# Seven block products in place of eight in the gate and up products of a feed-forward layer

## The chip, the cores and the metric

The kernel runs on one core of a Trainium2 chip. The metric is the device time of one execution in microseconds: the median of three runs before the change is 3075.05 us (3074.8 to 3081.02). TensorE (PE) multiplies; a weight load (PEld) brings the stationary operand into it. VectorE (DVE) and ScalarE (ACT) work on PSUM and SBUF; SyncE (SP) issues every DMA of this kernel, in one queue and in program order.

## The reference, cut to what matters

Two trunk layers run over 1072 token columns (32 of the sample group, 16 meta tokens, 1024 of the prompt). Each layer is a token mixer followed by a SwiGLU feed-forward part, both between norms:

```python
D_MODEL = 1024
D_FF = 2816                      # 22 tiles of 128 features
def swiglu(x, w_gate, w_up, w_down):
    return (jax.nn.silu(x @ w_gate) * (x @ w_up)) @ w_down
...
x = x + rmsnorm(mix.astype(x.dtype), norm_mix_post[l])
ff = swiglu(rmsnorm(x, norm_ffn_pre[l]), ffn_w_gate[l], ffn_w_up[l], ffn_w_down[l])
x = x + rmsnorm(ff.astype(x.dtype), norm_ffn_post[l])
```

Everything is float32. The reference computes in that precision, and the kernel keeps it by splitting each operand in two parts.

## The kernel before, in words

**Layout.** Features lie on the partitions, tokens along the free dimension. The 1072 tokens are cut into three blocks of 304, 384 and 384 columns (`BLKS`). The normalised input of a product lies in SBUF as a high and a low part, `xh` and `xl`, eight tiles of 128 features each (`KD = 8`); weights come from DRAM as units of 128x1024 numbers (`raw`, two buffers) and are split into `wh` (a copy on ACT, L57) and `wl` (a subtraction on DVE, L58). `mm3` (L154 to L156) makes one 128x128 by 128xN product as three matmuls: high by high, low by high, high by low.

**Storage.** 29 strips of 128x1072 numbers are handed out and taken back by the program. Eight PSUM banks serve the products in turn.

**Feed-forward.** The 22 tiles of hidden features are done in eleven groups (`FFG`): the first has 3 tiles, the second 1, the other nine 2 each. For a group, `ffn_gu` makes for each token block the gate product and the up product of a tile (8 x 3 matmuls each), takes the silu on ACT (L249), multiplies on DVE (L251) and splits the result into the strips `hid` (L170, L171). Then `kblock` multiplies the group's hidden tiles with their rows of the down weights and adds the results to the eight accumulator strips `acc` (L273 on DVE; L271 on ACT in the first group). One tile therefore costs 144 matmuls for gate and up and 72 for down.

**Ends of a layer.** In the last group each token block is finished with gate, up and down before the next one. `side(b, acc)` then queues the norm of that block: `postnorm` (squares summed on ACT and DVE, one matmul by ones, L178, an inverse root, then two DVE passes with the residual from DRAM) and, where another layer part follows, `prenorm` (the same again, ending in the split into `xh` and `xl`). Block order is 0, 1, 2, in the last layer 1, 2, 0 (`LAST`).

**Order of work.** A main generator emits the products; a `Driver` advances queued side generators (norms, scans, the sample states' updates) by a rate per step of the main one. Behind it a scheduler sets, when the program is built, each engine's final order. The sample states' update of a mixer (`later`: `even_samples`, `odd_samples`) runs beside the feed-forward part that follows it: per sample one load, a few DVE operations, one matmul (L1233), an addition (L1234), one store (L1235); in `odd_samples` there are 32 samples and two buffers for them.

Of the kernel before, what the change touches and what calls it, by code (L numbers as in the profile page):

```python
# [26 lines left out]


class Weights:
    """Ordered stream of [128, 1024] weight units, each split into two float32r parts."""  # L30

    def __init__(self, core, seq):
        self.core, self.seq = core, seq
        self.pos, self.done = 0, 0
        self.ready = {}
        self.reserve = 0
        self.raw = {}
        self.rpos = 0

    def _load(self):  # L40
        c = self.core
        src = self.seq[self.rpos]
        r = c.raw_p.tile([P, 4 * VA], F32, tag="raw", name="raw")[:, :src.shape[-1]]
        c.nc.sync.dma_start(out=r, in_=src)
        self.raw[self.rpos] = r
        self.rpos += 1

    def pump(self, limit):
        """Prepare units until `limit` are ready beyond those taken."""
        c = self.core  # L50
        while self.done < len(self.seq) and self.done - self.pos < limit and len(c.free) >= 2 + self.reserve:
            while self.rpos < len(self.seq) and self.rpos <= self.done:
                self._load()
            r = self.raw.pop(self.done)
            hi, lo = c.strip(F32R, "wh"), c.strip(F32R, "wl")
            w = r.shape[-1]
            c.nc.scalar.activation(out=hi.t[:, :w], in_=r, func=AF.Copy)  # L57
            c.nc.vector.tensor_tensor(out=lo.t[:, :w], in0=r, in1=hi.t[:, :w].bitcast(F32), op=ALU.subtract)  # L58
            self.ready[self.done] = (hi, lo)
            self.done += 1  # L60
            if self.rpos < len(self.seq) and self.rpos <= self.done:
                self._load()
# [10 lines left out]
    def pos_need(self):  # L73
        while len(self.core.free) < 2:
            self.core.D.force()
# [11 lines left out]
class Core:  # L87
    def __init__(self, ctx, tc, I, O):
# [18 lines left out]
        self.oh = self.dram.tile([P, 16, T], F32, name="oh")  # L107
        self.ol = self.dram.tile([P, 16, T], F32, name="ol")
# [17 lines left out]
    # storage  # L126
# [14 lines left out]
    def ps(self, n=512):  # L141
        tags = ["mm0", "mm1", "mm2", "kt", "sc", "a0", "a1", "o"][:self.nps]
# [4 lines left out]
    nps = 8  # L147
    tables = False

    # arithmetic  # L150
    def mm3(self, out, w, x, first, last):
        nc = self.nc
        (wh, wl), (xh, xl) = w, x
        nc.tensor.matmul(out, lhsT=wh, rhs=xh, start=first, stop=False)  # L154
        nc.tensor.matmul(out, lhsT=wl, rhs=xh, start=False, stop=False)  # L155
        nc.tensor.matmul(out, lhsT=wh, rhs=xl, start=False, stop=last)  # L156
# [16 lines left out]
    def rstd(self, ss, n, inv=None, eps=EPS):  # L173
        """rsqrt(mean + eps) on all partitions of the summed squares ss [128, n]."""
# [15 lines left out]
    def lnexp(self, after=None):  # L190
        """Load the table set that serves both Ln and Exp; placed behind `after`."""
# [18 lines left out]
    def prenorm(self, acc, b, w):  # L210
# [5 lines left out]
        for k in range(KD):  # L216
            xn = self.tmp(n)
# [21 lines left out]
    # feed-forward  # L239
    def ffn_gu(self, units, hid, b):  # L240
# [3 lines left out]
        for i in range(len(units) // 2):  # L244
            pg = self.proj(units[2 * i], b)
            yield
            pu = self.proj(units[2 * i + 1], b)
            sg = self.tmp(n)
            nc.scalar.activation(out=sg, in_=pg, func=AF.Silu)  # L249
            hd = self.tmp(n)  # L250
            nc.vector.tensor_tensor(out=hd, in0=sg, in1=pu, op=ALU.mult)  # L251
            self.split(hd, hid[2 * i].t[:, c0:c0 + n], hid[2 * i + 1].t[:, c0:c0 + n])
            yield
# [1343 lines left out]
```

## Time and profile before

| | |
|---|---|
| median of three runs | 3075.05 us |
| span of the profiled execution, first to last instruction (its own time: the page gives no other) | 3072.7 us |
| PE busy | 3005.9 us, 98% |
| DVE busy | 1717.4 us, 56% |
| ACT busy | 1174.9 us, 38% |
| DMA queue q1, share of 16 engines | 28.4% |
| mean granted clock of TensorE | 0.989 |
| feed-forward of the first layer, first gate product to last down product | about 607 to 1409 us |
| feed-forward of the second layer | about 2259 to 3055 us |

A PE row of the profile shows how long one matmul was in the array, from its start to its modelled end. Matmuls are pipelined, so the next one starts long before that end: what a matmul costs in a full stream is the distance from start to start, which the windows give as a stretch of time divided by the number of matmuls that started in it.

### The profile page before, as it was taken

What the parts mean: (1) busy time and instruction counts of PE and PEld (TensorE: products, weight loads), DVE (VectorE), ACT (ScalarE), POOL (GpSimd) and SP (SyncE); (2) the same over time, 40 slices, a digit from 0 to 9 for tenths busy, and PEclk for the clock granted to TensorE, in tenths of its full rate; (3) what the DMA queues carried; (4) which work ended last, traced back from release to release, by engine and by line L of the source; (5) the groups of instructions that cost most, each with busy time, mean ns of one, the idle gap of its engine ahead of it and who ended that gap; (6) DMA issues with size and microseconds to landing.
All of it is one profiled execution on the core that took longest, in us unless ns stands there. A gap on an engine that the chain in (4) does not pass through costs nothing.

```text
span 3072.7 us, 47149 instructions
## 1 busy us (share of the span) xinstructions
PE 3005.9 (98%) x19042; PEld 2897.2 (94%) x19042; DVE 1717.4 (56%) x3387; ACT 1174.9 (38%) x2442; POOL 9.2 (0%) x47
## 2 busy tenths in 40 slices
PE   7999999999999999998999999999999999999997
PEld 7998989999999999998988898989999999999996
DVE  7645545753444333368887787775482444454336
ACT  6533435542111111145667575854353111111113
POOL 0000000000000000000000000000000000000000
PEclk9999999999999999999999999999999999999998
DMA  4120216221211111113344444366332122222103
GB/s 140 42 72 29 79 67 202 96 83 49 83 69 62 49 49 55 43 58 113 99 131 125 130 135 139 117 210 216 132 117 76 55 83 83 83 90 84 54 15 115
DMA packets 180202, 286.38 MB, mean 93 GB/s; under 512 B 24944, under 2 KB 135952, under 8 KB 179984
## 3 DMA queue, kind: packets, MB, share of 16 engines
q1 hardware_dynamic: 179984, 283.37, 28.4%
q8 instruction: 149, 2.44, 0.3%
q14 instruction: 69, 0.57, 0.1%
HBM read 217.18 MB, written 66.14 MB: 92 GB/s over the span
## 4 chain that ended last, share of the span: by engine, by line
PE 89%; DVE 5%; ACT 2%; DMA 2%; issue 2%; SPq 0%; DVEq 0%; ACTq 0%
PE ps L154 26%; PE ps L155 25%; PE ps L156 25%; DMA cumb<-cum_d 1%; PE ps L524 1%; PE ps L526 1%; PE ps L525 1%; PE b_a L1131 1%; PE b_o L678 1%; PE b_a L1177 1%; PE b_o L1179 1%; DVE t L206 1%; PE b_o L675 1%; PE b_a L659 1%; DVE acc L235 1%
## 5 line engine op out<-in xcount | busy, mean ns | idle before, releaser
L154 PE MATMUL ps<-xh,wh 128*128 128x384 f32 (+1 forms) x4152 | 1371.8, 331 | 10.4 <-ACT xh L170 6.5
L155 PE MATMUL ps<-xh,wl 128*128 128x384 f32 (+1 forms) x4152 | 1362.0, 328 | 7.6 <-DVE wl L58 7.6
L156 PE MATMUL ps<-xl,wh 128*128 128x384 f32 (+1 forms) x4152 | 1360.7, 328 | 0.0
L154 PEld LDWEIGHTS ps<-xh,wh 128*128 128x128 f32 x4152 | 784.7, 189 | 29.1 <-issue 11.1
L155 PEld LDWEIGHTS ps<-xh,wl 128*128 128x128 f32 x4152 | 784.2, 189 | 15.4 <-DVE wl L58 8.8
L156 PEld LDWEIGHTS ps<-xl,wh 128*128 128x128 f32 x4152 | 783.7, 189 | 4.0 <-issue 1.7
L57 ACT ACTIVATE wh<-raw 128x1024 fp32r<-128x1024 f32 (+1 forms) x225 | 238.1, 1058 | 581.3 <-PE ps L156 357.0
L58 DVE TENSOR_TENSOR wl<-raw,wh 128x1024 fp32r<-128x1024 f32 (+1 forms) x225 | 273.7, 1223 | 250.1 <-ACT wh L57 133.1
L154 PE MATMUL ps<-hid,wh 128*128 128x384 f32 (+1 forms) x1056 | 346.2, 328 | 15.6 <-DVE t L251 7.8
L155 PE MATMUL ps<-hid,wl 128*128 128x384 f32 (+1 forms) x1056 | 345.0, 327 | 0.0
L156 PE MATMUL ps<-hid,wh 128*128 128x384 f32 (+1 forms) x1056 | 344.5, 327 | 0.0
L251 DVE TENSOR_TENSOR t<-t,ps 128x384 f32<-128x384 f32 (+1 forms) x132 | 69.2, 526 | 477.1 <-PE ps L156 474.5
L273 DVE TENSOR_TENSOR acc<-acc,ps 128x384 f32<-128x384 f32 (+1 forms) x480 | 235.8, 525 | 122.1 <-PE ps L156 121.9
L154 PEld LDWEIGHTS ps<-hid,wh 128*128 128x128 f32 x1056 | 200.0, 189 | 18.3 <-DVE t L251 9.2
L155 PEld LDWEIGHTS ps<-hid,wl 128*128 128x128 f32 x1056 | 200.0, 189 | 1.1
L156 PEld LDWEIGHTS ps<-hid,wh 128*128 128x128 f32 x1056 | 199.8, 189 | 0.1
L170 ACT ACTIVATE hid<-t 128x384 fp32r<-128x384 f32 (+1 forms) x132 | 65.9, 500 | 331.0 <-DVE t L251 330.9
L249 ACT ACTIVATE t<-ps 128x384 f32<-128x384 f32 (+1 forms) x132 | 61.5, 467 | 289.0 <-PE ps L156 288.9
L206 DVE TENSOR_TENSOR t<-t 128x384 f32<-128x384 f32 (+1 forms) x168 | 88.8, 529 | 24.7 <-ACT t L205 16.6
L1037 DVE SCALAR_TENSOR_TENSOR xs<-cv,o_convw,xs 128x1040 f32<-128x1040 f32 x72 | 93.4, 1299 | 14.0 <-ACT xs L1035 12.9
L171 DVE TENSOR_TENSOR hid<-t,hid 128x384 fp32r<-128x384 f32 (+1 forms) x132 | 69.7, 529 | 42.0 <-ACT hid L170 41.0
L205 ACT ACTIVATE t<-acc 128x384 f32<-128x384 f32 (+1 forms) x168 | 77.1, 496 | 41.6 <-DVE acc L1360 20.3
(275 smaller groups left out, 2840.5 us busy)
## 6 DMA issues: line engine op xcount, KB each, us to landing
raw<-in_wg SPq DMA_DIRECT2D x44, 512.0 KB, 3.2
raw<-in_wu SPq DMA_DIRECT2D x44, 512.0 KB, 3.3
raw<-in_wd SPq DMA_DIRECT2D x44, 512.0 KB, 3.2
cumb<-cum_d SPq DMA_DIRECT2D x32, 512.0 KB, 5.7
raw<-in_od_x SPq DMA_DIRECT2D x24, 512.0 KB, 3.5
oh<-t SPq DMA_DIRECT2D x48, 192.0 KB, 2.0
ol<-t SPq DMA_DIRECT2D x48, 192.0 KB, 2.2
xh<-oh SPq DMA_DIRECT2D x12, 768.0 KB, 5.8
```

The lines of the kernel that those rows point to most:

```text
L57: c.nc.scalar.activation(out=hi.t[:, :w], in_=r, func=AF.Copy)
L58: c.nc.vector.tensor_tensor(out=lo.t[:, :w], in0=r, in1=hi.t[:, :w].bitcast(F32), op=ALU.subtract)
L154: nc.tensor.matmul(out, lhsT=wh, rhs=xh, start=first, stop=False)
L155: nc.tensor.matmul(out, lhsT=wl, rhs=xh, start=False, stop=False)
L156: nc.tensor.matmul(out, lhsT=wh, rhs=xl, start=False, stop=last)
L170: self.nc.scalar.activation(out=hi, in_=src, func=AF.Copy)
L171: self.nc.vector.tensor_tensor(out=lo, in0=src, in1=hi.bitcast(F32), op=ALU.subtract)
L205: nc.scalar.activation(out=sq, in_=acc[k].t[:, c0:c0 + n], func=AF.Square)
L206: nc.vector.tensor_tensor(out=ss, in0=ss, in1=sq, op=ALU.add)
L251: nc.vector.tensor_tensor(out=hd, in0=sg, in1=pu, op=ALU.mult)
L273: nc.vector.tensor_tensor(out=a, in0=a, in1=ps, op=ALU.add)
L1037: nc.vector.scalar_tensor_tensor(out=out, in0=src(k), scalar=w[:, k:k + 1], in1=out, op0=ALU.mult, op1=ALU.add)
```

## The change

**Gate and up of 19 of the 22 tiles per layer** become one product of blocks. The gate tile and the up tile are stacked as two block rows; the 1024 input features are cut into even and odd tiles of 128 (two block columns of the weights, two block rows of the input); the tokens are cut into four stretches of `Q = 268`, of which a pair forms the two block columns of the result. The 2x2 by 2x2 block product is then made in seven products in place of eight, in the form with 15 additions: the weights appear as `a11`, `a12`, `a22` and the sums `s1` to `s4`, the input as three of its blocks in `xh`/`xl`, one quarter of it again (`s4`), and four sums `T`. `quad_gu` runs the seven forms; each form is 2 x 4 `mm3`, that is 24 matmuls of 268 columns, so a tile costs 168 of those in place of 144 matmuls of 304 or 384 columns.

**Weights.** `Weights` makes from each pair of raw units seven forms (`_form`): four DVE sums of 128x512, and for each form a high part on ACT and a low part on DVE, 128x512 each, in one strip. Seven forms are kept ahead.

**Input sums.** `prenorm` leaves the normalised input in the accumulator strips (`keep`), and `tforms` makes 16 strips of sums from them, queued behind the norm of the last block. The first three tiles (`PLAIN`) are done in the old way.

**Results.** Products that share summands accumulate in one PSUM bank: six banks (two each of `qa`, `qe`, `qb`), read by DVE between two forms (L376), or by ACT. Two banks (`kt`, `sc`) are left to the side work.

**Hidden tiles through DRAM.** Each hidden tile is split and written to `oh` and `ol` (`spill`), and read back into rows of `xh` and `xl` (`fetch`, L468) once the gate and up products no longer need them. The down products then run after all gate and up products, in K blocks of 2, 4, 4, 4, 4 and 4 tiles (`DOWN`). `later` is queued when the seven-product stage starts, and drained at its end.

```diff
+FORMS = ("a11", "s1", "s2", "s4", "s3", "a12", "a22")
+Q = 268
...
+    def _form(self, f, raws):
...
+        if f == "s1":
+            combine("s1", blocks["a21"], blocks["a22"], ALU.add)
+            combine("s2", sums["s1"], blocks["a11"], ALU.subtract)
+        elif f == "s4":
+            combine("s4", blocks["a12"], sums["s2"], ALU.subtract)
+        elif f == "s3":
+            combine("s3", blocks["a11"], blocks["a21"], ALU.subtract)
+        w, src = c.strip(F32R, "w_" + f), sums.get(f, blocks.get(f))
+        hi, lo = half(w)
+        nc.scalar.activation(out=hi, in_=src, func=AF.Copy)
+        nc.vector.tensor_tensor(out=lo, in0=src, in1=hi.bitcast(F32), op=ALU.subtract)
...
-            self.split(hd, hid[2 * i].t[:, c0:c0 + n], hid[2 * i + 1].t[:, c0:c0 + n])
+        self.spill(i, c0, n, hd)
...
+    def tforms(self, acc):
...
+            combine(0, b12, b11)
+            combine(1, b22, r[0])
+            parts(0, 0)
+            yield
+            combine(0, b21, r[1])
+            parts(1, 1)
+            yield
+            combine(1, b22, b12)
+            parts(3, 0)
+            yield
+            parts(2, 1)
...
+        for f in FORMS:
+            (w,), = W.take(1)
+            x = {"a11": "a", "a12": "a", "s1": "e", "s4": "e"}.get(f, "b")
+            for tb in range(2):
+                ps = bank[x, tb]
+                for j in range(4):
+                    s = slice(j * P, j * P + P)
+                    t = slice(512 + j * P, 512 + j * P + P)
+                    self.mm3(ps, (w.t[:, s], w.t[:, t]), self.right(f, j, tb), f in ("a11", "s1", "s2") and j == 0,
+                             f in ("a12", "s4", "a22") and j == 3, skip_group_check=True)
+                if f == "a11":
+                    nc.scalar.activation(out=s1[tb], in_=ps, func=AF.Copy)
+                elif f == "s1":
+                    add(s15[tb], ps, s1[tb])
+                elif f == "s2":
+                    s2[tb] = self.tmp(Q)
+                    add(s2[tb], ps, s1[tb])
+                elif f == "s4":
+                    sg[tb] = self.tmp(Q)
+                    add(sg[tb], ps, s2[tb])
+                    nc.scalar.activation(out=sg[tb], in_=sg[tb], func=AF.Silu)
+                elif f == "s3":
+                    hd = self.tmp(Q)
+                    add(hd, ps, s15[tb])
+                    add(hd, hd, sg[tb], ALU.mult)
+                    self.spill(i, (2 * tb + 1) * Q, Q, hd)
+                elif f == "a12":
+                    sg[tb] = self.tmp(Q)
+                    nc.scalar.activation(out=sg[tb], in_=ps, func=AF.Silu)
+                else:
+                    hd = self.tmp(Q)
+                    add(hd, ps, s1[tb])
+                    add(hd, hd, sg[tb], ALU.mult)
+                    self.spill(i, 2 * tb * Q, Q, hd)
+            self.drop(w)
...
+            W.pump(7)
...
+        for i in range(PLAIN, 22):
+            yield from self.quad_gu(W, i, (lambda: fetch(0)) if i == 21 else None)
+        D.drain()
...
+        for c, t in enumerate(tiles):
+            dn = W.take(len(t))
+            if c + 1 < len(tiles):
+                fetch(c + 1)
...
+            for k, b in enumerate(order if last else range(3)):
+                for _ in self.kblock(dn, rows, acc, b, c == 0):
+                    yield
+                if last:
                     side(b, acc)
...
-FFG = (3, 1) + (2,) * 9
+PLAIN = 3
+DOWN = (2, 4, 4, 4, 4, 4)
```

The order of the instructions shows two places that the prediction speaks of. The first is DVE, in the first layer, where the gate and up products of the first three tiles end (L251 before and L311 now multiply the silu with the up product, `ps` being its PSUM bank). Before, the low parts of coming weight units (L58) stood between these products:

```order
L171 TENSOR_TENSOR hid1_6385<-t_6930,hid0_6384 128x384
L58 TENSOR_TENSOR wl_7055<-raw_6708,wh_7054 128x1024
L251 TENSOR_TENSOR t_6986<-t_6984,ps_6959 128x384
L58 TENSOR_TENSOR wl_7149<-raw_7058,wh_7148 128x1024
L171 TENSOR_TENSOR hid3_6387<-t_6986,hid2_6386 128x384
```

Now the end of the input sums (L333 makes a sum in `traw`, L338 its low part in a strip `t1` to `t4`) and then the sums and low parts of the first weight forms (L82, L94) stand there:

```order
L338 TENSOR_TENSOR t2_6997<-traw_6707,t2_6997 128x536
L311 TENSOR_TENSOR t_7034<-t_7032,ps_7007 128x384
L333 TENSOR_TENSOR traw_6707<-acc7_5449,acc6_5448 128x536
L226 TENSOR_TENSOR t_7037<-t_7034,t_7036 128x384
L338 TENSOR_TENSOR t4_6999<-traw_6707,t4_6999 128x536
L338 TENSOR_TENSOR t3_6998<-traw_6707,t3_6998 128x536
L82 TENSOR_TENSOR sums_7108<-raw_6368 128x512
L82 TENSOR_TENSOR sums_7108<-sums_7108,raw_6362 128x512
L94 TENSOR_TENSOR w_a11_7109<-raw_6362,w_a11_7109 128x512
L94 TENSOR_TENSOR w_s1_7114<-sums_7108,w_s1_7114 128x512
L94 TENSOR_TENSOR w_s2_7117<-sums_7108,w_s2_7117 128x512
```

So 32 DVE operations of 128x536 for the input sums and the forms' first operations now stand ahead of the first seven-product tile.

The second is SP in the second layer. Before, the loads and stores of the samples (L1226, L1235; `ssm` is their strip) stood among the loads of weight units (L44):

```order
L44 DMA raw_25795<-in_wg1 128x1024
L1235 DMA out_ss_s<-ssm_23053 128x512
L44 DMA raw_25872<-in_wu1 128x1024
L1226 DMA ssm_23053<-in_ss_in 128x512
L44 DMA raw_25878<-in_wd1 128x1024
L44 DMA raw_26078<-in_wd1 128x1024
```

Now, where the seven-product stage ends, the last of them (L1406 loads, L1415 stores) stand among the reads of the hidden tiles for the second K block (L468):

```order
L500 DMA ol_83<-t_28717 128x268
L1406 DMA ssm_23840<-in_ss_in 128x512
L468 DMA xl_76<-ol_83 128x1072
L1406 DMA ssm_23840<-in_ss_in 128x512
L468 DMA xh_75<-oh_82 128x1072
L1415 DMA out_ss_s<-ssm_23840 128x512
```

What moved here is a remainder of `later`: 13 of the 32 sample products of the second layer stand behind the last seven-product tile, between the first down products.

More of the change, by code (lines that the diff above doesn't have):

```diff
@@ new lines, in need, with combine @@
+    def need(self):
+        return 2 if self.items[self.done][0] == "unit" else 1
+    def _form(self, f, raws):
+        c, nc = self.core, self.core.nc
+        blocks = {}
+        for r, row in zip(raws, "12"):
+            if r in self.raw:
+                w = self.raw[r].rearrange("p (j e m) -> p j e m", j=4, e=2)
+                blocks |= {f"a{row}1": w[:, :, 0], f"a{row}2": w[:, :, 1]}
+        half = lambda w: [w.t[:, o:o + 512].rearrange("p (j m) -> p j m", j=4) for o in (0, 512)]
+        sums = dict(zip(("s1", "s2", "s4", "s3"), 2 * half(c.sums))) if f[0] == "s" else {}
+        def combine(f, x, y, op):
+            nc.vector.tensor_tensor(out=sums[f], in0=x, in1=y, op=op)
+        if f == "s1":
[9 more added lines that the diff above has]
+        nc.vector.tensor_tensor(out=lo, in0=src, in1=hi.bitcast(F32), op=ALU.subtract)
+        return w
@@ L237, in postnorm, with ffn_gu, ffn_gu_tile @@
             yield
-    def ffn_gu(self, units, hid, b):
+    def ffn_gu(self, units, b):
+        for i in range(len(units) // 2):
+            yield from self.ffn_gu_tile(units[2 * i:2 * i + 2], i, b)
+    def ffn_gu_tile(self, units, i, b):
         nc = self.nc
@@ L257, in kblock @@
+    def kblock(self, units, rows, acc, b, first):
         nc = self.nc
@@ new lines, in ffn @@
+        gu = W.take(2 * PLAIN)
+        for b in range(3):
+            if b < 2:
+                yield from self.ffn_gu(gu, b)
+                continue
+            for i in range(PLAIN):
+                for _ in self.ffn_gu_tile(gu[2 * i:2 * i + 2], i, b):
+                    yield
+                for u in gu[2 * i:2 * i + 2]:
+                    self.drop(*u)
+                if i == PLAIN - 1:
+                    D.need(("tf", 0))
+                    self.keep, self.sums = self.strip(F32, "keep"), self.strip(F32, "sums")
+                    W.pump(7)
@@ new lines, in ffn @@
+        D.drain()
+        self.pstags = None
+        self.drop(self.keep, self.sums, *sum(self.T, []))
+        acc = [self.strip(F32, f"acc{k}") for k in range(KD)]
+        for c, t in enumerate(tiles):
+            dn = W.take(len(t))
+            if c + 1 < len(tiles):
+                fetch(c + 1)
+            rows = [row(i) for i in t]
+            last = c + 1 == len(tiles)
+            for k, b in enumerate(order if last else range(3)):
+                for _ in self.kblock(dn, rows, acc, b, c == 0):
+                    yield
+                if last:
```

201 lines of the change are left out of this document (120 added, 81 removed).

## Prediction

> **What bounds the kernel now.** I read the page's busy times and its chain of waits first, then windows of single stages, because the price of a matmul can only be seen where PE streams.
>
> ```profile
> PE 3005.9 (98%) x19042; PEld 2897.2 (94%) x19042; DVE 1717.4 (56%) x3387; ACT 1174.9 (38%) x2442; POOL 9.2 (0%) x47
> PE 89%; DVE 5%; ACT 2%; DMA 2%; issue 2%; SPq 0%; DVEq 0%; ACTq 0%
> L154 PE MATMUL ps<-xh,wh 128*128 128x384 f32 (+1 forms) x4152 | 1371.8, 331 | 10.4 <-ACT xh L170 6.5
> ```
>
> PE is busy 98% of the span, and the chain that ended last runs over PE for 89% of it. The 331 ns of the third row are not the price of a matmul: they reach from its start to its modelled end, and the next one starts meanwhile. The price is the step from start to start. Three windows lie in streams of one width (264 columns, 304, 384), a fourth holds one whole group of two feed-forward tiles; the first figure after the window is its length, the first (x) counts matmuls.
>
> ```profile
> 82.50:91.10 8.60, 8.60 (x72) 8.60 (x71) 6.19 (x14) 5.90 (x15) 0.00 (x0) 1.00 0.17 61
> 679.70:689.40 9.70, 9.70 (x72) 9.70 (x71) 2.16 (x3) 3.04 (x7) 0.00 (x0) 1.00 0.17 57
> 690.00:714.00 24.00, 24.00 (x139) 24.00 (x138) 0.99 (x1) 8.43 (x16) 0.00 (x0) 1.00 0.00 1
> 1083.38:1154.07 70.69, 70.69 (x433) 70.69 (x433) 25.10 (x42) 11.97 (x18) 0.00 (x0) 1.00 0.13 45
> ```
>
> Since a matmul is drawn about two steps long, two of each of the first three counts had begun before the window. The steps are 8.60/70 = 122.9 ns for 264 columns, 9.70/70 = 138.6 ns for 304 and 24.00/137 = 175.2 ns for 384: close to proportional to the columns (0.46 ns each). The group takes 70.69 us for its 432 matmuls, PE busy throughout, DVE busy a third of it. So inside the feed-forward part the time is PE's column count.
>
> **The seven products.** A tile's gate and up are 288 of the group's 432 matmuls, halved for one tile, with the same mix of widths: 70.69 x 2/3 / 2 = 23.56 us. For 38 tiles that is 895.3 us. The built program has 6384 matmuls of 268 columns (38 x 168). Their step is not in the trace; the nearest row is 264 columns, 122.9, and by the slope to 304 (15.7 ns over 40 columns) four columns add 1.6: I take 124.5. 6384 x 124.5 = 794.8 us, which removes **100.5 us**. Bounds: 122.9 (the narrower row) gives 110.7 us, 138.6 (the wider row) 10.5 us.
>
> The down products stay 72 matmuls a tile; samples, mixers and norms keep their matmuls. So all else is a matter of cover.
>
> **DVE and ACT in a seven-product tile.** A tile lasts 168 x 124.5 = 20.9 us. Beside it DVE has 11 operations of 128x512 (four sums, seven low parts) and 18 of 128x268 (14 additions and products, four low parts), ACT seven of 128x512 and ten of 128x268. Priced by the rows of 512, and of 304 for 268 (too dear, if anything):
>
> ```profile
> L1182 DVE TENSOR_TENSOR ST<-ST,cd 128x512 f32<-128x512 f32 x32 | 21.9, 685 | 0.1
> L251 DVE TENSOR_TENSOR t<-t,ps 128x304 f32<-128x304 f32 x44 | 20.7, 470 | 128.7 <-PE ps L156 126.1 <-ACT wh L57 2.6
> L1112 ACT ACTIVATE ek<-cumb 64x512 f32<-64x512 f32 x64 | 40.2, 628 | 36.6 <-DVE xs L1188 23.9 <-DMA cumb<-cum_d 11.9
> L170 ACT ACTIVATE hid<-t 128x304 fp32r<-128x304 f32 x44 | 20.1, 458 | 91.6 <-DVE t L251 91.6
> ```
>
> DVE: 11 x 0.685 + 18 x 0.470 = 16.0 us; ACT: 7 x 0.628 + 10 x 0.458 = 9.0 us. Both fit. The waits are tighter: bank `qb` takes s2, s3 and a22, and `qe` s1 and s4, with one form in between, so from the last matmul of a form's first token half to the next use of that bank lie the other half and one form, 36 x 124.5 ns = 4.5 us, in which one DVE addition has to run. The heaviest form (s3: six operations of 268, two of 512) is 4.2 us of DVE per 3.0 us of PE; the lighter forms around it give that back. I book 0 for these waits. Their price without that cover is the second rival. The eight stores and two loads per tile are ten issues on SP:
>
> ```profile
> raw<-in_wg SPq DMA_DIRECT2D x44, 512.0 KB, 3.2
> oh<-t SPq DMA_DIRECT2D x24, 152.0 KB, 1.8
> xh<-oh SPq DMA_DIRECT2D x12, 768.0 KB, 5.8
> ```
>
> Loads land in 3.2 us and forms are made a tile ahead: nothing. The first K block's 144 down matmuls (two thirds of the 35.3 us that one tile costs, 23.6 us) cover eight reads of 536 KB for the next; reads of 768 KB land in 5.8 us and overlap: nothing in the first layer.
>
> **Before the first tile of each layer.** DVE must end the last norm, make the input sums (32 operations of 128x536, by the 512 row and its 1.05 ns per column 0.71 us each, 22.7 us), the last five or so L311/L226 pairs (1.1 us each, 5.5) and three operations for a11 (2.1): 30.3 us. What time is there:
>
> ```profile
> 646.88 1.01 DVE L171 TENSOR_TENSOR xl<-t,xh 128x384 fp32r<-128x384 f32 x2
> 679.62 0.30 PE L154 MATMUL ps<-hid,wh 128*128 128x304 f32 x1
> 2304.46 0.56 DVE L171 TENSOR_TENSOR xl<-t,xh 128x384 fp32r<-128x384 f32 x1
> 2330.81 0.30 PE L154 MATMUL ps<-hid,wh 128*128 128x304 f32 x1
> ```
>
> From the norm's last low part to the end of the three tiles' gate and up: 31.7 us in the first layer, 25.8 in the second. I book 0 and **5 us**; the ends are 0 and 20 (each of the 16 sums waiting 0.6 us for its ACT copy in both layers).
>
> **Between the layers.** The last group of before covers the norms of its own token blocks with gate, up and down; now the last K block covers them with down alone.
>
> ```profile
> 1338.80:1440.00 101.20, 90.76 (x516) 87.30 (x514) 81.52 (x175) 55.27 (x108) 0.78 (x7) 0.95 0.36 113
> 1394.89 0.69 PE L154 MATMUL ps<-hid,wh 128*128 128x384 f32 x1 [6.67 <-ACT t L249]
> 3048.50:3053.50 5.00, 4.94 (x18) 4.73 (x19) 2.67 (x7) 2.28 (x5) 0.00 (x0) 0.50 0.22 79
> ```
>
> From block 0's last down product to block 2's second mean square the norms take 101.2 us, DVE busy 81.5, and PE loses 10.4 us idle. In the new order the same two landmarks hold 312 matmuls of 384 and 144 of 304, 312 x 0.1752 + 144 x 0.1386 = 74.6 us. DVE loses the eight L251/L171 operations (0.55 each) and the waits on them; by its own chain the norms then need about 91 us. PE waits 91 - 75 = 16 us in place of about 14 (idle and slowed): **3 us**, ends 0 and 25. After the last block of the kernel only the last norm runs, now as before: 0.
>
> The third row is a stretch after a 3.8 us wait: the granted clock is 0.50. The Trainium skill ("TensorE: Matmul & The Clock Gate", What's actually happening) says the same, half clock after an idle window of about 3.4 us; by it each long wait here would cost some 2 us more, which lies within the ends given.
>
> **The samples' remainder in the second layer.** 13 sample products stand behind the last seven-product tile. Two buffers, each turn being store, load, product, matmul, addition:
>
> ```profile
> out_ss_s<-ssm SPq DMA_DIRECT2D x32, 256.0 KB, 2.0
> ssm<-in_ss_in SPq DMA_DIRECT2D x32, 256.0 KB, 2.6
> L1230 DVE TENSOR_TENSOR ssm<-ssm,cd 128x512 f32<-128x512 f32 x32 | 21.9, 688 | 21.7 <-DMA ssm<-in_ss_in 21.7
> L1233 PE MATMUL ps<-bxs 96*128 96x512 f32 x32 | 12.7, 397 | 0.0
> ```
>
> 2.0 + 2.6 + 0.7 + 0.4 + 0.7 and some 0.4 between them is 6.8 us a turn, 3.4 us a sample. Ten of them stand ahead of the 124th down matmul, which PE reaches in 72 x 0.1386 + 51 x 0.1752 + 10 x 0.4 = 23 us; ten samples take 34. Behind them on SP wait the hidden tiles' reads, and for these PE's second K block. **11 us**; ends 0 and 35 (loads as slow as the 5.8 us of the row of larger reads).
>
> **Sum.** 3072.7 - 100.5 + 5 + 3 + 11 = 2991.2 us of span. The median of the runs is 2.3 us above the profiled span, so **2993.5 us**, 2.7% faster.
>
> **Rivals.** *Stage ends cost their upper bounds* (20 + 25 + 35 = 80 in place of 19): 3072.7 - 100.5 + 80 + 2.3 = 3054.5. For it: DVE is already the pace of the norms (81.5 of 101.2 us). Against: three upper ends at once.
>
> *PSUM banks come back late (slower).* If DVE, in order, keeps PE waiting at each form:
>
> ```profile
> 1360.62 0.44 PE L154 MATMUL ps<-hid,wh 128*128 128x384 f32 x1 [0.83 <-DVE t L251]
> ```
>
> 0.83 us, where DVE was late in the last group, times 266 forms is 221 us: 3214. It decides from (100.5 - 19)/266 = 0.31 us a form. For it: DVE is loaded to 77% of a tile, more with samples. Against: 4.5 us of slack, and forms are interleaved with additions one by one.
>
> *A matmul costs mostly a fixed part.* If 268 columns took the 138.6 ns of 304, 884.8 us would stand against 895.3, and with 19 us of stage ends the result is 3083.5, slower. Against: three widths lie on one line. The Trainium skill (same page, Back-to-back issue gap) gives about 81 ns at 128 columns and 131 at 512 for streams of load and matmul. That line would give 99 ns at 268 and 111 for the old mix, and make 1.17 times as many matmuls 4% dearer, some 39 us on gate and up; the rows here are steeper, and they decide.
>
> That the change does less than it says is excluded by the count of 6384.
>
> **Chances.** Forecast, 2964 to 3030: 0.80. Stage ends dearer, 3030 to 3068: 0.10. Late banks: 0.06. Fixed part: 0.02. A gain lost to within 0.2%: 0.02. About 0.2% (6 us) is what a measurement of this kernel can tell. Faster: 0.80 + 0.10 + 0.01 of the others' mild ends = 0.91; same 0.03; slower 0.06. The lower end is 110.7 us removed with all stage ends at nothing, 3072.7 - 110.7 + 2.3 = 2964; the upper end, 3030, is 37 us more of stage ends.
>
> **What would show it.** Right: in a window over one seven-product tile, about 124.5 ns a step, with 20.9 us a tile and PE busy throughout; idle PE of 5, 16 and 11 us at the three places, the last with the samples' products (L1413) as the waiting instruction. Wrong: waits of PE on L376 in every form; a step above 130 ns; DVE busy above 19 us a tile; or long waits for L468's reads in the first layer, which I booked at nothing.

## The result and the profile after

The changed kernel takes 3002.65 us (median of four executions, 2992.85 to 3010.77) against 3074.93 us before: a ratio of 0.976, 95% interval 0.9736 to 0.9784. Its profiled execution has a span of 2991.1 us and is the shortest of the four.

The page of the changed kernel, busy times and the chain of waits by engine:

```profile
PE 2898.7 (97%) x19954; PEld 2786.3 (93%) x19954; DVE 1962.2 (66%) x4009; ACT 1297.9 (43%) x2811; POOL 9.3 (0%) x47
PE 86%; DVE 5%; DMA 4%; ACT 2%; issue 2%; SPq 0%; DVEq 0%; ACTq 0%
```

There are 912 more matmuls and 107 us less of busy PE: each of the new ones is narrower than those it replaces. DVE has gained 245 us, as an engine beside the path. The chain still runs over PE.

Windows over the two stages of seven products, from the first matmul of 268 columns to the last, and the 32 us ahead of the second of them (columns as before: length, then busy time and count of PE, PEld, DVE, ACT, POOL; then granted clock, DMA share, GB/s):

```profile
674.01:1071.80 397.79, 397.79 (x3209) 397.09 (x3209) 292.92 (x578) 152.19 (x322) 0.00 (x0) 1.00 0.41 132
2282.12:2682.94 400.82, 398.85 (x3212) 397.21 (x3212) 294.91 (x607) 146.67 (x323) 0.00 (x0) 1.00 0.43 138
2250.00:2282.00 32.00, 32.00 (x184) 32.00 (x183) 31.34 (x55) 17.34 (x32) 0.00 (x0) 1.00 0.16 57
```

The first stage holds 3192 matmuls of 268 columns and 16 products of the samples (0.24 us each): (397.79 - 3.8) / 3192 = 123.4 ns a step. A tile takes 20.9 us with its sample products (397.79 / 19), PE without a gap; DVE is busy 15.4 us of it and ACT 8.0. The second stage is 3 us longer; two waits of about 1 us are in it. Ahead of it PE does not wait, but DVE is busy 31.3 of 32 us.

The three ends of stages that the prediction priced: the norms between the layers, from the last down product of block 0 to the second mean square of block 2; the down products behind the last seven-product tile of the second layer; and the end of the program behind the last down product.

```profile
1297.10:1394.30 97.20, 82.31 (x467) 78.78 (x466) 74.74 (x159) 47.07 (x97) 0.61 (x6) 0.93 0.29 93
2684.00:2760.00 76.00, 66.16 (x364) 61.53 (x365) 41.41 (x68) 20.46 (x36) 0.00 (x0) 0.91 0.76 265
2965.40:2991.10 25.70, 1.64 (x4) 0.50 (x2) 18.96 (x42) 5.91 (x11) 0.00 (x0) 0.59 0.48 158
```

PE's waits in the first two of them, as the view of waits lists them (engine, what waited, for what: us in total, times, longest):

```profile
PE b_sc L233 <- DVE t L261: 10.1, 2, 9.9
PE ps L209 <- DVE t L240: 7.4, 3, 2.6
...
PE ps L1413 <- DVE ssm L1414: 4.6, 2, 2.5
PE ps L209 <- ACT wh L107: 2.4, 1, 2.4
PE ps L209 <- DVE t L376: 2.3, 1, 2.3
```

The third wait for L240, 2.6 us at the odd mixer's first product, stands just behind the stretch between the layers. In both places the granted clock is below 1 (0.93, 0.91): part of the matmuls behind the longer waits run at half speed. In the second, a matmul of a sample (L1413) waits for the addition of an earlier one (L1414), and the DMA engines are busy 76% of the time.

What each stretch loses beyond its matmuls can be worked out: its length less the count of matmuls of each width times its step (123.4, 139.5 and 175.5 ns for 268, 304 and 384 columns, streams of both traces give 140 and 175.5 for the last two; 240 ns for a sample's, some 0.15 us for one of a mean square). The 24 us between the layers run to the odd mixer's first product, 100.7 us in all, of which 74.8 are 312 matmuls of 384 and 144 of 304 columns. PE is idle 17.5 of these 24 us and 9.8 of the 17 at the samples; the rest is matmuls at half clock and changes from one width to another. Of the mixers only the difference between the two kernels has a meaning, since their narrow matmuls are priced roughly.

| us of PE | before | after | change | predicted |
|---|---|---|---|---|
| gate and up of 38 tiles | 895.3 | 787.8 | -107.5 | -100.5 |
| ahead of the first seven-product tile, two layers | 0 | 0 | 0 | +5 |
| inside the tiles | 0 | 2 | +2 | 0 |
| norms between the layers | 16 | 24 | +8 | +3 |
| samples' remainder, second layer | 0 | 17 | +17 | +11 |
| end of the program | 27 | 28 | +1 | 0 |
| even mixer | | | -6 | 0 |
| odd mixer | | | +2 | 0 |

The sum is -83.5, the spans differ by 81.6; the rest is the rounding of the steps.

### The profile page after: what moved, and what is told of

It is laid out like the page before. It is cut to its first block, busy times and chain, and to the rows that moved or that the text cites. A ratio compares the mean times of both kernels' runs of the same rounds, so it can differ in the third digit from the quotient of the medians.

```text
span 2991.1 us, 51345 instructions
## 1 busy us (share of the span) xinstructions
PE 2898.7 (97%) x19954; PEld 2786.3 (93%) x19954; DVE 1962.2 (66%) x4009; ACT 1297.9 (43%) x2811; POOL 9.3 (0%) x47
## 4 chain that ended last, share of the span: by engine, by line
PE 86%; DVE 5%; DMA 4%; ACT 2%; issue 2%; SPq 0%; DVEq 0%; ACTq 0%
PE ps L209 17%; PE ps L210 17%; PE ps L211 16%; PE qb L211 4%; PE qb L210 4%; PE qb L209 3%; PE qe L211 2%; PE qe L209 2%; PE qe L210 2%; PE qa L209 2%; PE qa L210 2%; PE qa L211 2%; DMA cumb<-cum_d 2%; PE ps L704 1%; PE ps L706 1%
## 5 line engine op out<-in xcount | busy, mean ns | idle before, releaser
L209 PE MATMUL ps<-xh,wh 128*128 128x384 f32 (+1 forms) x3384 | 1123.9, 333 | 24.7 <-DVE t L240 8.9
L210 PE MATMUL ps<-xh,wl 128*128 128x384 f32 (+1 forms) x3384 | 1111.0, 328 | 7.9 <-DVE wl L108 7.8
L211 PE MATMUL ps<-xl,wh 128*128 128x384 f32 (+1 forms) x3384 | 1109.2, 329 | 0.0
L209 PEld LDWEIGHTS ps<-xh,wh 128*128 128x128 f32 x3384 | 640.8, 189 | 50.0 <-DVE t L240 11.5
L211 PEld LDWEIGHTS ps<-xl,wh 128*128 128x128 f32 x3384 | 640.0, 189 | 3.6 <-issue 1.7
L435 DVE TENSOR_TENSOR acc<-acc,ps 128x384 f32<-128x384 f32 (+1 forms) x240 | 120.1, 525 | 224.3 <-PE ps L211 224.0
L225 ACT ACTIVATE t<-t 128x268 fp32r<-128x268 f32 (+2 forms) x194 | 86.1, 444 | 227.1 <-DVE t L376 136.5
L209 PE MATMUL qa<-xh,w_a 128*128 128x268 f32 x608 | 174.0, 286 | 1.0 <-ACT t L405 1.0
L210 PE MATMUL qb<-t,w_s 128*128 128x268 f32 x608 | 174.1, 286 | 0.0
L210 PE MATMUL qa<-xh,w_a 128*128 128x268 f32 x608 | 173.9, 286 | 0.0
L211 PE MATMUL qb<-t,w_s 128*128 128x268 f32 x608 | 173.8, 286 | 0.0
L211 PE MATMUL qa<-xl,w_a 128*128 128x268 f32 x608 | 173.7, 286 | 0.0
L209 PE MATMUL qb<-t,w_s 128*128 128x268 f32 x608 | 173.5, 285 | 0.0
L93 ACT ACTIVATE w_s<-sums 128x512 fp32r<-128x512 f32 x152 | 95.2, 627 | 152.1 <-DVE sums L82 103.7
L209 PEld LDWEIGHTS qa<-xh,w_a 128*128 128x128 f32 x608 | 114.3, 188 | 1.2 <-ACT t L405 1.2
L210 PEld LDWEIGHTS qa<-xh,w_a 128*128 128x128 f32 x608 | 114.5, 188 | 0.5
L210 PEld LDWEIGHTS qb<-t,w_s 128*128 128x128 f32 x608 | 114.3, 188 | 0.4
L209 PEld LDWEIGHTS qb<-t,w_s 128*128 128x128 f32 x608 | 114.3, 188 | 0.2
```

The lines of the kernel that those rows point to most:

```text
L93: nc.scalar.activation(out=hi, in_=src, func=AF.Copy)
L225: self.nc.scalar.activation(out=hi, in_=src, func=AF.Copy)
L435: nc.vector.tensor_tensor(out=a, in0=a, in1=ps, op=ALU.add)
```

## Experiments

Ratios are to runs of the kernel before on the same chip. It took 3074.3 us beside the first four experiments, 3070.5 beside the next four and 3072.9 beside the last two, so differences in microseconds between these groups are good to some 4 us.

**The same kernel again.** Nothing is edited.

> The changed kernel once more, unaltered. Its four timed executions lie between 2992.9 and 3010.8 us, 18 us apart, and the profiled one (2991.1 us of span) is the shortest of them. Theory: the quads and the ends of the stages take the same time in every execution, and the scatter is a granted clock that falls to half at some short waits of the even mixer in one execution and not in another: windows over a seven-product tile again 20.9 to 21.0 us, the samples' remainder again 17 us, and the first matmul after each norm of the even mixer shifted in steps of 1 to 4 us against the first profile. Rival: the additional time is in the feed-forward parts (their DMA traffic meets other traffic): tiles above 21.2 us or PE waits in them.

Measured: 3002.24 us (2995.96 to 3005.99), ratio 0.9768, interval 0.975 to 0.9786. The first stage of seven products took 397.8 us again, each of its 19 tiles within 0.01 us of the first profile; the samples' remainder and the end were the same too. What differs stands in the mixers. The same stretch of the even mixer in the changed kernel and in its repetition, then a later one in the changed kernel and in the kernel of the third experiment, whose mixer is the same code:

```profile
243.00:251.00 8.00, 7.68 (x32) 5.43 (x30) 4.30 (x14) 2.02 (x7) 0.00 (x0) 0.50 0.14 51
...
243.00:251.00 8.00, 7.64 (x52) 6.03 (x50) 6.36 (x17) 3.42 (x10) 0.00 (x0) 1.00 0.14 52
...
355.00:360.00 5.00, 3.98 (x27) 3.60 (x28) 4.20 (x15) 2.41 (x8) 0.99 (x1) 1.00 0.37 135
...
355.00:360.00 5.00, 4.47 (x23) 3.40 (x23) 2.60 (x8) 0.66 (x2) 0.99 (x1) 0.50 0.42 144
```

The granted clock is 0.50 in one execution and 1.00 in the other: 32 matmuls in 8 us against 52. Each such fall costs some 4 us (the repetition is 3.7 us ahead behind the first place). So the first theory holds as to the kind of thing that scatters, but not as to the even mixer alone. The repetition starts its first seven-product tile at 671.3 us, 2.7 us ahead of the first profile (674.0), and is 3.1 us longer in all: from the end of that stage to the start of the second one it takes 1216.0 us in place of 1210.1, with more falls of the clock in the odd mixer. The changed kernel's slower executions left no trace; their clocks over the span (0.984 to 0.986, against 0.989) point the same way. Against the kernel before, 6 of the 81.6 us are falls that its even mixer had and the changed kernel's had not. The medians, 72 us apart, rest on four executions each and carry less of such luck.

**Eight products, the rest of the change kept.**

```diff
-            s += [g[i], u[i]] if i < PLAIN else [(g[i], u[i])]
+            s += [g[i], u[i]]
...
-            yield from self.quad_gu(W, i, (lambda: fetch(0)) if i == 21 else None)
+            gu = W.take(2)
+            for b in range(3):
+                for _ in self.ffn_gu_tile(gu, i, b):
+                    W.pump(4)
+                    yield
+                if i == 21:
+                    c0, n = BLKS[b]
+                    fetch(0, slice(c0, c0 + n))
...
```

> All 22 tiles as eight block products (the old gate and up), with the rest of the change kept: hidden tiles through DRAM, down products after all of gate and up in K blocks of 2 and 4, no sums of inputs or weights. It tells the seven products from the rearrangement. Theory: a tile costs 23.5 us again in place of 20.95, 38 x 2.6 = 99 us more than the changed kernel, about 3090 to 3100 us, so 15 to 25 us slower than the kernel before: the price of the rearrangement alone. Rival: the rearrangement pays by itself (K blocks of 4 read the accumulators less often); then this kernel takes 3075 us or less.

Measured: 3126.26 us, ratio 1.0173, interval 1.0158 to 1.0189: 124 us slower than the changed kernel, not 99, and 52 slower than before. Neither expectation holds. The tiles took 23.6 us without sample products, as expected (23.5). In the profiled executions, 136 us apart, the 19 tiles of the first layer take 54.1 us more than with seven products, so both layers some 108; most of the rest lies behind the last tile of the second layer:

```profile
PE ps L1416 <- DVE ssm L1417: 15.1, 5, 5.8
PE ps L1416 <- DVE bxs L1411: 8.5, 10, 2.0
PE ps L209 <- DVE ssm L1417: 5.3, 1, 5.3
...
2790.00:2832.00 42.00, 13.06 (x24) 5.36 (x23) 19.60 (x34) 1.12 (x2) 0.00 (x0) 0.57 0.88 296
```

16 sample products (L1416) stand in a row there with nothing between them, and 42 us hold 24 matmuls: some 22 us more than the changed kernel loses there. The end of the program, from the last down product on, was 2.6 us longer (28.3 in place of 25.7). So this kernel did not measure the rearrangement alone, but with the remainder of the samples in a worse place; the last experiment but one takes it up again.

**The samples spread over the whole stage.**

```diff
-RATE = [1.2, 1.2, 1.5, 1.5, 1.5, 6.5, 6.0, 0.3, 1.25]
+RATE = [1.2, 1.2, 1.5, 1.5, 1.5, 6.5, 6.0, 0.5, 1.25]
```

> One number: the samples' update is advanced 0.5 in place of 0.3 steps per form, so that it is emitted whole beside the seven-product tiles and nothing of it stands behind the last one. Theory: PE's loss of 17 us in the first 76 us of the second layer's down products (2684 to 2760 us) goes, 14 to 17 us faster than the changed kernel, and the tiles stay at 20.9 to 21.0 us, DVE busy some 0.7 us more per tile. Rival 1: the reads of the hidden tiles (eight of 536 KB per K block) are what PE really waits for there; then a wait for L468 takes the place and less than 5 us is gained. Rival 2: the samples take DVE in the tiles from the bank additions; then L376 waits of PE appear and the tiles get longer by about as much.

Measured: 2989.01 us, ratio 0.9723, interval 0.9701 to 0.9744: 13.6 us faster than the changed kernel. Windows of its second layer, the seven-product stage and the 76 us behind it:

```profile
2294.50:2700.90 406.40, 403.60 (x3225) 400.73 (x3225) 312.97 (x644) 148.38 (x325) 0.00 (x0) 1.00 0.48 152
2701.00:2777.00 76.00, 75.34 (x465) 74.83 (x464) 26.72 (x42) 21.30 (x36) 0.00 (x0) 1.00 0.63 230
```

PE starts 465 matmuls in those 76 us, not 364, at full clock, though the reads of the hidden tiles are there as before. So the samples were the cause, and the first rival falls. The stage itself is 5.6 us longer: 13 sample products of 0.24 us have moved into it (3.1 us), and PE waits for additions of DVE a little more often. That is the small share of the second rival.

**The last two K blocks together, token block by token block.**

```diff
-        for c, t in enumerate(tiles):
+        for c, t in enumerate(tiles[:-2]):
...
-            for k, b in enumerate(order if last else range(3)):
+            for k, b in enumerate(range(3)):
                 for _ in self.kblock(dn, rows, acc, b, c == 0):
                     yield
-                if last:
-                    side(b, acc)
...
+        x, y, z = order
+        for h, b in ((0, x), (0, y), (1, x), (1, y), (0, z), (1, z)):
+            for _ in self.kblock(*ends[h], acc, b, False):
+                yield
+            if h:
+                side(b, acc)
...
```

> The last two K blocks are done together, token block by token block, so that behind the norm of the first block there are 67 us of down products in place of 34, and behind the second 34 in place of 17. Theory: the norms between the layers take about 91 us of DVE's own chain; the 24 us that PE loses there fall to 0 to 5 us. In the last layer DVE is done with the second norm before the last down product, so the end behind the last down product falls from 25.8 us to about 18. Together 20 to 28 us faster than the changed kernel. Rival: DVE is the pace through the odd mixer's first products as well; the wait only moves there (PE waits on L226 or L261 at the first products of the odd mixer) and less than 8 us is gained.

Measured: 2975.7 us, ratio 0.9685, interval 0.9659 to 0.9711: 26.9 us faster than the changed kernel. The largest wait of PE between the layers, and the end of the program:

```profile
PE ps L209 <- DVE acc L435: 7.7, 1, 7.7
...
2953.00:2970.70 17.70, 1.74 (x5) 0.62 (x3) 11.17 (x27) 4.07 (x8) 0.00 (x0) 0.58 0.41 131
```

The end fell from 25.7 to 17.7 us, as expected. Between the layers the loss is 15 us in place of 24: PE now waits for one addition of a K block (L435), which stands on DVE behind eight pairs of norm operations (L288, L290). The cover was there, the order on DVE was not. These two places make 17 of the 26.9 us. The profiled executions lie 20.4 us apart, of which 4.4 stand in the even mixer, whose code is the same; what is left of the 26.9 us is not told from scatter.

**Three edits together.** The samples at 0.5, the joint K blocks, and the norms between the layers advanced more slowly:

```diff
-                D.add(gen(), RATE[5], ("xn", b))
+                D.add(gen(), 2.5 if w == 3 else RATE[5], ("xn", b))
...
```

> Three edits together: the samples advanced 0.5 steps per form, the last two K blocks done token block by token block, and the norms between the layers advanced 2.5 steps per step of the main work in place of 6.5, so that the additions of the K blocks do not stand behind eight pairs of norm operations on DVE (in the kernel with the joint K blocks PE waits 7.7 us there for one addition, L435). Theory: the places do not share a cause, so the gains add: 3002.6 - 13.6 - 26.9 - 5 to 8 us, 2952 to 2960 us. Rival: DVE has no room left where the norms stand; what is taken from the K blocks comes back in the odd mixer's first products, and the sum ends at 2965 us or above.

Measured: 2956.67 us (2951.53 to 2961.3, five executions), ratio 0.9631, interval 0.9618 to 0.9645: 46.0 us faster than the changed kernel by the medians, 40 by the ratios (41.4 between the profiled executions), and 113.8 us faster than the kernel before beside it. The first two edits made 40.5 us one by one; what the slower norms add is too small to be read from these medians. The same two stretches as before, and the 9.3 us behind the first of them:

```profile
1276.50:1376.70 100.20, 99.93 (x588) 97.63 (x586) 81.80 (x176) 49.94 (x101) 0.93 (x7) 1.00 0.34 110
1376.70:1386.00 9.30, 4.63 (x14) 3.59 (x15) 6.42 (x13) 5.72 (x12) 0.00 (x0) 0.82 0.00 0
2701.00:2777.00 76.00, 76.00 (x467) 76.00 (x467) 29.01 (x48) 9.56 (x9) 0.00 (x0) 1.00 0.34 126
```

PE has no gap left in the two stretches, and the norms take 100 us as before. They were never made faster; they are covered, but not to their end: right behind the stretch PE waits 4.6 us for the first high part of the last block (L225), at the odd mixer's first products. With the clock's fall behind it the loss between the layers is 8 us, against 24 in the changed kernel and 15 with the joint K blocks. So a small share of the rival came true. Within the scatter the gains add, and the traces show them in separate places, so the causes are separate.

**One plain tile less.**

```diff
-PLAIN = 3
+PLAIN = 2
```

> PLAIN = 2 in place of 3: one more tile per layer in seven products, one less ahead of them. The input sums are made beside the plain tiles, and DVE is busy 31.3 of the 32 us ahead of the first seven-product tile in both layers. Theory: that cover is used to the last microsecond; two tiles less of 23.6 us of PE's work bring 5.2 us by the product count, but PE then waits for the sums about 20 us per layer (23.6 less the 3 us of the removed tile's own DVE operations): some 30 to 37 us slower than the changed kernel. Rival: the sums would also be ready earlier if they were asked for earlier, the bound is only their place in the order; then within 5 us or 5 us faster.

One execution: 3023.8 us, 21 us above the changed kernel's median (its span 31 us above the profiled one). PE's waits ahead of the first seven-product tiles, of the first layer and then of the second:

```profile
PE qe L209 <- ACT w_s L93: 11.9, 1, 11.9
PE ps L209 <- DVE t L240: 3.6, 1, 3.6
...
PE qe L209 <- ACT w_s L93: 4.4, 1, 4.4
PE ps L209 <- DVE t L240: 4.1, 1, 4.1
```

PE waits for a weight form (L93) that is made behind the input sums, and the clock falls with it (0.85 over the 56 us around the first place, 0.90 over 50 us around the second). So the cover of the third plain tile is needed. The size, from one execution, is below the 30 to 37 us that were expected.

**A loaded DVE.** Tiles get 0 to 4 idle operations behind each form, three tiles each:

```diff
+            for _ in range((0, 1, 2, 3, 4, 0)[(i - 3) // 3 if i < 21 else 5]):
+                nc.vector.tensor_tensor(out=self.junk, in1=self.junk, op=ALU.max, in0=(
+                    {"a11": s1, "s1": s15, "s2": s2, "s4": sg, "a12": sg}.get(f) or [None, hd])[1][:, :256])
...
```

> The changed kernel with idle operations on DVE behind each form (a maximum of 128x256, estimated 0.42 us by the row of 268 columns, its result unused): none in tiles 3 to 5, one per form in 6 to 8, two in 9 to 11, three in 12 to 14, four in 15 to 17, none behind. It prices the waits for PSUM banks that were booked at nothing. Theory: DVE is busy 15.1 of a tile's 20.95 us and has 4.5 us for each bank; one operation (18.0 us per tile) costs nothing, two (20.9) next to nothing, three (23.8) and four (26.8) make DVE the pace: tiles of about 20.95, 21, 23.8, 26.8 us. Rival: the order of the banks decides, not the sum; then each operation of 0.42 us lengthens every form, tiles of 23.9, 26.8, 29.8, 32.7 us, from the first operation on.

One execution, 3024.9 us. Windows over three tiles each in the first layer, with 0, 1, 2, 3 and 4 operations:

```profile
679.28:742.22 62.94, 62.94 (x509) 62.80 (x509) 46.21 (x92) 23.83 (x52) 0.00 (x0) 1.00 0.40 127
742.22:805.25 63.03, 63.03 (x509) 62.73 (x507) 53.82 (x112) 22.97 (x50) 0.00 (x0) 1.00 0.40 131
805.25:870.75 65.50, 64.30 (x509) 63.17 (x509) 58.54 (x132) 22.78 (x52) 0.00 (x0) 1.00 0.36 115
870.75:937.59 66.84, 64.89 (x510) 63.28 (x509) 64.66 (x151) 22.98 (x49) 0.00 (x0) 1.00 0.33 105
937.59:1005.26 67.67, 64.88 (x511) 63.26 (x510) 67.03 (x164) 23.20 (x49) 0.00 (x0) 1.00 0.33 101
```

The first operation per form costs 0.03 us a tile, with DVE busy 85% of the time; so the banks have slack, and the rival falls. Two cost 0.9 us a tile at 89%, three and four 1.3 and 1.6 us at 97 and 99%. The steps of 23.8 and 26.8 us did not come. An idle operation is drawn 0.42 us long, as estimated, but on a full DVE the next operation starts 0.34 us after it, so drawn lengths add up to more than DVE needs; and 17 of the 210 operations trailed behind the last window. PE begins to wait a little before DVE is full, and DVE's sum then sets the pace.

**Half the columns per matmul.**

```diff
-                    self.mm3(ps, (w.t[:, s], w.t[:, t]), self.right(f, j, tb), f in ("a11", "s1", "s2") and j == 0,
...
+                    m = 2 if i in (10, 13) else 1
+                    for h in range(m):
+                        z = slice(h * Q // m, (h + 1) * Q // m)
+                        self.mm3(ps[:, z], (w.t[:, s], w.t[:, t]), [a[:, z] for a in self.right(f, j, tb)],
+                                 f in ("a11", "s1", "s2") and j == 0,
...
```

The second half starts its sums anew in the same bank, so the values of these two tiles change; the number and the shape of the matmuls are as told.

> The changed kernel, but in tiles 10 and 13 each product of 268 columns is made as two of 134, into the two halves of the same bank: twice the matmuls, the same columns. It measures the fixed part of a matmul alone. Theory (cost in proportion to the columns, 0.46 ns each, at most the line through 264 and 304 columns, 0.39 ns): 61 to 72 ns a step, a tile of 336 matmuls in 20.7 to 24.2 us. Rival: a fixed part shows at this width, from the matmul or from the load of its weights, and the step stays above 80 ns: tiles above 27 us. The Trainium skill (TensorE: Matmul & The Clock Gate, Back-to-back issue gap) gives about 81 ns at 128 columns, 27.5 us by it.

One execution, 3062.4 us. A stretch inside tile 10:

```profile
830.00:855.00 25.00, 25.00 (x225) 24.95 (x225) 13.80 (x24) 5.45 (x11) 0.00 (x0) 1.00 0.21 72
```

25 us hold 223 steps of 112 ns. A tile takes 37.7 to 38.0 us for 336 matmuls, both tiles and both layers alike, where the theory allowed 24.2. So proportional cost is wrong at this width: there is a floor. By the Trainium skill (TensorE: Matmul & The Clock Gate, Back-to-back issue gap), which gives about 81 ns for 128 columns, some 81 ns would have been seen; the row is 38% above.

**Eight products with the ends covered.** The fastest kernel, but with eight products for all tiles (the edit of the second experiment) and the samples at 0.6.

> Eight block products again for all tiles, but with the three edits of the fastest kernel so far (samples advanced 0.6 steps per step so that none stand behind the last tile, last two K blocks token block by token block, norms advanced 2.5 steps). The first kernel with eight products took 3126 us, of which 41 us were a pile of sample products behind the last tile and 27 us the end of the program. Theory: those were ends of stages and not the rearrangement as such; with the ends covered the difference to the fastest kernel (2956.7 us) is the seven products alone, 38 x 2.6 to 2.75 = 99 to 104 us: 3055 to 3062 us, tiles of 23.6 us, 10 to 15 us faster than the kernel before. Rival: hidden tiles through DRAM and separate down products cost time by themselves; then 3090 us or more.

Measured: 3057.82 us, ratio 0.996, interval 0.9947 to 0.9973. One tile with its two sample products:

```profile
697.65:721.72 24.07, 24.07 (x147) 23.98 (x146) 8.90 (x12) 4.88 (x9) 0.00 (x0) 1.00 0.40 134
```

24.07 less 0.48 is 23.6 us. The difference to the fastest kernel is 101 us, the seven products alone: in the profiled executions the two stages of 19 tiles differ by 54.1 and 52.6 us, out of 105.9 in all; the rearrangement with covered ends is 8 to 16 us faster than the kernel before, by the interval. What the first kernel with eight products lost was ends of stages.

**Other cuts of 268 columns.**

```diff
+                    for z in {10: (slice(0, 180), slice(180, Q)), 13: (slice(0, 88), slice(88, 178), slice(178, Q)),
+                              16: (slice(0, 224), slice(224, Q))}.get(i, (slice(0, Q),)):
+                        self.mm3(ps[:, z], (w.t[:, s], w.t[:, t]), [a[:, z] for a in self.right(f, j, tb)],
+                                 f in ("a11", "s1", "s2") and j == 0 and not z.start,
...
```

> The changed kernel, but in tile 10 each product of 268 columns is made as 180 + 88 columns, in tile 13 as 88 + 90 + 90, in tile 16 as 224 + 44. Two of 134 each took 112 ns a step, not 61 to 72, so there is a floor. Theory A, the floor is per matmul with its load of 128x128 weights and does not depend on the columns: every step of 44, 88, 90, 180 and 224 columns is 112 ns, tiles of 37.7, 56.5 and 37.7 us. Theory B, narrow matmuls cost 0.84 ns a column (112/134): steps of 151, 74 and 76 ns for 180, 88 and 90 columns and 188 and 37 ns for 224 and 44; tiles of about 37.8 us whatever the cut.

One execution, 3220.4 us. A window over tile 10 and four through tile 13 in the first layer, and one over tile 13 in the second:

```profile
815.90:853.60 37.70, 37.70 (x340) 37.66 (x338) 18.00 (x33) 8.45 (x18) 0.00 (x0) 1.00 0.31 101
...
895.60:900.00 4.40, 4.40 (x43) 4.40 (x41) 2.17 (x5) 1.51 (x4) 0.00 (x0) 1.00 0.85 243
900.00:905.00 5.00, 5.00 (x28) 5.00 (x27) 1.38 (x2) 0.16 (x1) 0.00 (x0) 0.55 0.27 101
905.00:915.00 10.00, 10.00 (x49) 10.00 (x48) 1.13 (x2) 0.91 (x2) 0.00 (x0) 0.50 0.00 0
915.00:999.50 84.50, 84.50 (x395) 84.37 (x395) 11.76 (x23) 6.13 (x13) 0.00 (x0) 0.50 0.05 17
...
2622.50:2725.60 103.10, 103.10 (x507) 103.00 (x506) 18.07 (x36) 8.54 (x18) 0.00 (x0) 0.52 0.11 34
```

Tiles 10 and 16 took 37.4 to 37.7 us, and the weight loads of both stand 111 to 112 ns apart whatever the columns (44, 88, 180, 224), as do those of the first 4.4 us of tile 13. (Where the width changes, the drawn start of a matmul jumps, so that single steps of 37 to 190 ns stand in the trace of tile 16; the loads, and the steps among matmuls of 88 and 90 columns, do not show this.) The times of tiles 10 and 16 fit both theories; the steps decide. Theory A holds as to the floor: by theory B, at 0.84 ns a column, matmuls of 88 and 90 columns would step at 74 to 76 ns, and they step at 112. But tile 13 took 103.9 us in the first layer and 103.1 in the second, and not 56.5, for a reason that neither theory had; it stands in the last section.

## Why the prediction held, and which terms were off

The predicted 2993.5 us lies 9 us below the median, inside the range. The profiled span (2991.1) agrees with the sum (2991.2) by more luck than the terms deserve: the errors of the terms cancel, and this execution is the shortest of the four. None of the signs of being wrong that the prediction named came. Of its signs of being right, idle PE of 5, 16 and 11 us at the three places, PE shows 0, 14.9 (97.20 less 82.31) and 9.8 (76.00 less 66.16).

- **The seven products** (-100.5). Right. 268 columns took 123.4 ns, not 124.5, below the chosen value and above the lower bound: 7 us more. The two kernels that differ in the products alone are 101 us apart.
- **DVE and the banks** (0). Right: 15.4 us of DVE in a tile, the samples' operations included (16.0 booked without them), no waits in the first layer, 2 us in the second. The rival of late banks falls by the loaded DVE: one more operation per form cost nothing.
- **Ahead of the first tile** (0 and 5, ends 0 and 20). 0 and 0. DVE was busy 31.3 of the 32 us, so the end at 20 was near; with one plain tile less PE waits.
- **Between the layers** (+3). The mechanism was right, the size too small: +8. The step that failed is "the norms then need about 91 us". They took 97.2, of which DVE was busy 74.7 and waited 12.2 for ACT (L239); so DVE's busy time does not set the length, the chain of ACT and DVE operations does, and taking eight operations away shortened it by 4 us and not by 10. PE's half clock is not needed for that: in the three edits together, with PE busy throughout at 1.00, the norms took 100.2 us. (The prediction's 16 us in place of 14 are also 2 more, not 3.) The joint K blocks and the slower norms covered most of it.
- **The samples' remainder** (+11). Right in kind, 17 in size. The mis-sized terms are the landings, which were taken from rows of a quiet stage. In the crowded one they are, from the view of DMA issues between 2670 and 2780 us:

```profile
out_ss_s<-ssm SPq DMA_DIRECT2D x14, 256.0 KB, 3.1
ssm<-in_ss_in SPq DMA_DIRECT2D x12, 256.0 KB, 3.7
```

3.1 + 3.7 + 2.2 is 9.0 us a turn in place of 6.8, 4.5 us a sample; the 13 products stand 4.4 us apart (2683.1 to 2736.3 us). Ten of them would be 45 us against 23 of PE's work, 22 us; 17 were lost. PE's wait on the samples' own matmuls (L1413) is only 4.6 us of it; the other idle 5.2 us stand before down products. They share the cause all the same, since the loss falls to 1 us when the samples are moved (75.34 of 76.00 us busy).
- **The end of the program and the reads of the hidden tiles in the first layer** (0). Right: +1 and no wait.
- **What was not in the sum**: the even mixer, 6 us shorter in the profiled execution by its clock alone, and 2 us more in the odd one. The sum was made against one execution before; a median of the changed kernel should have been given some 5 to 10 us for that.
- **The fixed part of a matmul**, held at 0.02 because three widths lie on a line. At 268 columns that was right. The line does not go on: at 112 ns it meets a floor, by estimate near 112 / 0.46 = 243 columns (no width between 224 and 256 was run). The kernel's 268 lie 10% above it, so the rival was nearer than the three rows could tell.

## What to carry to other kernels

A product count that falls by an eighth brings that eighth only where the narrower matmuls stay above the floor of a matmul and its weight load, so price the new width by measuring it, and look on both sides of it. The rearrangement that it needs moves work to the ends of stages: here a side job that is drained late (17 us) and norms with too little work beside them (8 us more than before) took back a quarter of the 107.5 us, and rates and the order of blocks brought most of it back. Take a DMA's landing time from a stage as crowded as the one it will stand in.

## What the hardware showed

**A floor of 112 ns.** Matmuls of 44 to 224 columns, each with its load of 128x128 weights, step at 112 ns on the mean. Whether the load or the matmul sets it was not told apart. The Trainium skill (TensorE: Matmul & The Clock Gate, LDWEIGHTS (loading the stationary operand)) gives a load its column count over 1.2 GHz, 107 ns for 128 columns; the measured step is 5% above that, which speaks for the load but does not show it.

**Half clock in a stream without gaps.** In tile 13 of the last experiment PE waits for nothing that the trace shows, and after 4.9 us of matmuls of 88 to 90 columns the granted clock falls to 0.50 and stays there until the wide matmuls of the next tile have run some 3 us; the step becomes 213 ns. The same tile of the second layer does the same. Cuts of 134 and 134, of 180 and 88 and of 224 and 44 columns keep the clock at 1.00 at the same 112 ns a step. So not only an idle engine loses the clock: here the array moved 90 columns per 112 ns, against 134 on the mean in the others. That this share decides is a reading of these four cuts; no other was run. The Trainium skill (TensorE: Matmul & The Clock Gate, What's actually happening) ties the clock to how busy the engine has been in a window of 3.4 us; the row shows that a full queue does not count as busy by itself.

**A clock by chance.** The same instructions of the even mixer ran at 0.50 in one execution and at 1.00 in another, some 4 us each time. By the same section of the Trainium skill that window runs free of the program, which would explain it. The traces fit: in the records of the granted clock of all twelve, every stretch at one clock that ends inside the trace lasts a whole multiple of 3.41 us (in the changed kernel 3.41, 10.24 and 13.65 at half clock), and the fall at this place begins at 241.0, 241.8 or 242.8 us, in three of them, though their programs stand within 0.5 us of each other there. That the place of the window alone decides whether the clock falls is not shown. The fastest and the slowest execution lie 18 us apart in the changed kernel and 10 in the fastest one, as much as an end of a stage is worth; the traced executions show falls of the clock as the cause of such differences, the others left none.
